# First norm of a fused mixer and expert block: its factor folded into the router's weights, its mean taken off the logits, its scale and shift applied when tokens are gathered

## The chip, the cores and the metric

The kernel runs on one core of one Trainium2 chip. The metric is the device time of one execution, in microseconds (us). Below, PE is the matrix engine, DVE the vector engine, ACT the scalar engine, POOL the general engine, and SP the engine whose queue issues most transfers. A core has 16 DMA engines.

## The reference

Two transformer blocks on 256 tokens of width 1024, all in float32. The change touches the first norm of the first block, the router that reads it and the experts that take their tokens from it:

```
h = layer_norm(ALPHA * x + mix, ln1_g, ln1_b)          # mix = concat(attn, sgu) @ w_out + b_out
logits = h @ w_router + b_router                       # 32 experts
top 4 of the logits per token; gates = softmax over the four
expert e: gt = min(h_e @ w_gate[e] + b_gate[e], 7), up = clip(h_e @ w_up[e] + b_up[e], -7, 7)
          y_e = (gt * sigmoid(1.702 gt) * (up + 1)) @ w_down[e] + b_down[e]
x2 = layer_norm(ALPHA * h + sum of gate * y_e, ln2_g, ln2_b)   # then the second block
layer_norm(r, g, b) = (r - mean) * rsqrt(var + 1e-5) * g + b
```

## The kernel before, in words

The schedule is written by hand: each engine executes its instructions in the order of the code, and waits are put in where a tile is not ready. `front` is the first mixer with the router, `moe` the experts, and a second block follows.

**Weights of the front.** `pieces` and `pump` bring weights in through a ring of raw slots. A piece is split into two float32r parts, a high part cast by ACT (L1324) and the low rest, a subtraction of two SBUF tiles on DVE or POOL (L1325). There are four half slots: when PE has used a half, `freed` gives the slot back and `pump` emits the cast and the subtraction of the next half at once, so that these stand in ACT's and DVE's order where `freed` is called. The matrix `w_out` comes as eight halves, four for output columns 0 to 511 (`wo0`) and four for 512 to 1023 (`wo1`). The `wo1` halves go into the slots that the `wo0` halves leave.

**The end of the front.** `out_half` multiplies one half for the given token tiles (t is 0 or 1, 128 tokens each): `wo0` for both tiles, `wo1` for t=0 at 512 columns, then `wo1` for t=1 twice at 256 columns (q is 0 and 256). `evict` adds the product to the residual `r` (it is `self.h`) and takes statistics. `norm` subtracts the mean and multiplies by `ln1_g` in place and computes the reciprocal root `rs` in small DVE steps. `turned` transposes a tile of `r` on PE and copies it to `hT`. `by_experts` multiplies `hT` (or one column of it) by the router's weights, `ist` sums four partial results, and `router` forms the logits, their top 8 and the normed tokens `self.x`, with `ln1_b` added by POOL (L578).

**Expert biases.** `split_biases` is a generator in three stages that turns the gate and up biases, loaded into `bf`, into three bfloat16 parts `bgu`: an ACT copy of 2048 columns and a POOL subtraction; two ACT copies that need that subtraction and a second POOL subtraction; one last ACT copy. `hT` lies in the same memory as `bf`, so the transposed rows can be written only when all three stages are over.

**Experts.** 32 experts, weights streamed through a ring of nine tiles of 2 MB that is full when `moe` begins. `gather` multiplies the tokens by one-hot columns for two experts at a time and copies the result from PSUM to `xg`, half by DVE (L756), half by ACT (L757). `start_sum`, after the third expert's gate and up, starts the accumulator with ALPHA times the tokens plus the gated `b_down`. `scatter` adds the experts' results; its first two products need the PSUM banks that the gather before it used.

The lines around the change's first loop are these:

```
        for i in range(4):
            out_half(po, range(NT), i, self.parts("wo0"))
            freed()
            if i == 0:
                next(biases, None)
        c4 = by_experts(lambda k: bqs[:, 10 + k:11 + k], 1, V.tensor_copy)
        for t in range(NT):
            evict(t, 0, po[t])
        next(biases, None)
```

Of the kernel before, what the change touches and what calls it, by code (L numbers as in the profile page):

```python
# [12 lines left out]
F32 = mybir.dt.float32  # L13
# [4 lines left out]
OP = mybir.AluOpType  # L18
# [21 lines left out]
WARM = 12, 10, 11, 20  # L40
# [31 lines left out]
class Net:  # L72
# [66 lines left out]
    def run(self):  # L139
# [30 lines left out]
        self.top = pb.tile([128, NT, 8], F32, name="top")  # L170
        with ExitStack() as fctx:
            self.front(fctx)
# [28 lines left out]
    def front(self, fctx):  # L201
# [41 lines left out]
        bst = fp.tile([18, 128], F32, name="bst")  # L243
        nc.scalar.dma_start(bst[0:10, :], b_in[0:1280].rearrange("(r c) -> r c", c=128))
        nc.scalar.dma_start(bst[10:18, :], a["ln1_b"].rearrange("o (r c) -> (o r) c", c=128))
# [69 lines left out]
        p = bank("o", [128, 18])  # L315
# [5 lines left out]
        bqs = fp.tile([128, 18], F32, name="bqs")  # L321
# [207 lines left out]
        wr, ln1g, ln1b = L["wr"], L["ln1g"], L["ln1b"]  # L529
        lst = [f2.tile([128, 4, 6], F32, tag="lst", name=self.nm("lst")) for _ in range(NT)]  # L530

        def by_experts(rhs, n, E):

            p = bank("s", [128, n])
            for k in range(KC):
                j = k % 4
                self.mm(p[32 * j:32 * j + 32, :], wr[:, k, :], rhs(k), start=k < 4, stop=k >= 4)
            o = f2.tile([128, n], F32, tag=f"le{n}", name=self.nm("le"))
            E(o, p)
            return o  # L540

        cb = fp.tile([128, NE], F32, name="cb")

        bf = L["bf"]
# [7 lines left out]

        def norm(t):

            mv = f2.tile([128, 2], F32, tag="lmv", name=self.nm("lmv"))
            V.bn_aggr(mv, lst[t])
# [6 lines left out]
        def turned(t):  # L563
            for c0 in (0, 4):
                p = bank("s", [128, 4, 128])
                for c in range(4):
                    self.tr(p[:, c, :], r[:, t, (c0 + c) * 128:(c0 + c + 1) * 128])
                S.copy(hT[:, c0:c0 + 4, t * 128:(t + 1) * 128], p)

        def router(t, rs):  # L570
            le = by_experts(lambda k: hT[:, k, t * 128:(t + 1) * 128], 128, S.copy)
            p = bank("s", [128, NE])
            self.mm(p, le, ist)
            V.scalar_tensor_tensor(self.lg[:, t, :], p, rs, cb, op0=OP.mult, op1=OP.add)
# [34 lines left out]
        for q in (0, 256):  # L609
            p = bank("mm", [128, 256])  # L610
            for i in range(4):
                out_half({1: p}, (1,), i, self.parts("wo1", 0 if q else i), slice(q, q + 256))
                if q:
                    freed()
                    if i == 1:
                        turned(0)
# [1441 lines left out]
```

## Time and profile before

| | us |
|---|---|
| median of 3 runs | 1551.1 (1549.34 to 1552.4) |
| profiled execution, its own time | 1553.83 |
| span of the profiled execution | 1552.2 |
| PE busy | 1430.2 (92% of the span) |
| DVE busy | 613.9 (40%) |
| ACT busy | 365.4 (24%) |
| POOL busy | 179.3 (12%) |

The span runs from the first to the last instruction of the one profiled execution; times in the rows below count from its start. Busy shares are means over stages that differ: the front takes about the first 124 us, the experts' weights are streamed from there to about 1035 us, and the second block fills the rest. In the rows "idle before <- X" names what ended the engine's wait. [...]

### The profile page before, as it was taken

The numbers are of one execution on the slowest core, as the hardware profiler recorded it, in microseconds if no ns is written. First come the engines' busy times: TensorE is split into PE (matmuls) and PEld (weight loads), VectorE is DVE, ScalarE is ACT, GpSimd is POOL, SyncE is SP. The second block draws the span as 40 slices with busy tenths as digits, with TensorE's granted clock in tenths as the row PEclk, the third lists the DMA queues.
The fourth block names the chain that finished last, engine by engine and source line by source line (L and its number), as shares of the span: only waits on it lengthen the run. The fifth ranks groups of instructions, "written<-read, shape, count | busy, mean of one in ns | idle before, by whom it ended". The sixth has DMA issues, their size and how long they took to land. (4 is left out here: it accounts for less than half of the span.)

```text
span 1552.2 us, 19103 instructions
## 1 busy us (share of the span) xinstructions
PE 1430.2 (92%) x7944; PEld 830.2 (53%) x7944; DVE 613.9 (40%) x1087; ACT 365.4 (24%) x607; POOL 179.3 (12%) x155
## 2 busy tenths in 40 slices
PE   8789899999999989999998989897998999999998
PEld 7674333333333333333233233237877777799998
DVE  5882131222122122122124122126597547876664
ACT  4551100010110100100100110113643323365452
POOL 4630000000000011000000000004352223200000
PEclk9999989999999999999999999998988999999999
DMA  9887999999999999999999999983423124765530
GB/s 301 286 332 293 426 409 408 428 427 427 429 427 428 428 425 421 427 429 427 429 426 428 427 427 428 428 334 116 136 89 119 32 86 169 241 220 186 195 136 28
DMA packets 94510, 491.13 MB, mean 316 GB/s; under 512 B 13639, under 2 KB 44039, under 8 KB 67284
## 3 DMA queue, kind: packets, MB, share of 16 engines
q1 hardware_dynamic: 93536, 489.01, 78.2%
q8 instruction: 64, 1.05, 0.3%
q10 hardware_dynamic: 372, 0.66, 0.1%
q0 software_dynamic: 512, 0.20, 0.1%
q14 instruction: 26, 0.21, 0.0%
HBM read 488.34 MB, written 1.51 MB: 316 GB/s over the span
## 5 line engine op out<-in xcount | busy, mean ns | idle before, releaser
L89 PE MATMUL g<-w,xg 128*64 128x512 f32 x1024 | 239.0, 620 | 6.2 <-DMA w<-in_w_gate_dram 6.2
L89 PE MATMUL u<-w,xg 128*64 128x512 f32 x1024 | 227.1, 594 | 13.6 <-DMA w<-in_w_up_dram 13.6
L89 PE MATMUL y<-w,hidT 128*64 128x512 f32 x1024 | 226.9, 595 | 2.9 <-DMA w<-in_w_down_dram 1.7
L89 PEld LDWEIGHTS u<-w,xg 128*64 128x64 f32 x1024 | 70.8, 137 | 159.4 <-issue 132.6
L89 PEld LDWEIGHTS g<-w,xg 128*64 128x64 f32 x1024 | 74.5, 143 | 150.9 <-issue 137.7
L1324 ACT CAST w<-w 128x1024 fp32r<-128x1024 f32 (+1 forms) x116 | 118.7, 1035 | 148.8 <-PE pj L89 62.0
L89 PEld LDWEIGHTS y<-w,hidT 128*64 128x64 f32 x1024 | 70.8, 137 | 152.7 <-issue 144.8
L1325 POOL TENSOR_TENSOR w<-w,w 128x1024 fp32r<-128x1024 f32 (+1 forms) x33 | 79.5, 2413 | 587.8 <-ACT w L1324 582.5
L1325 DVE TENSOR_TENSOR w<-w,w 128x1024 fp32r<-128x1024 f32 x83 | 114.0, 1390 | 83.6 <-ACT w L1324 83.6
L823 ACT COPY y<-y 64x512 f32<-64x512 f32 x64 | 37.1, 579 | 369.8 <-PE y L89 369.4
L801 DVE TENSOR_SCALAR g<-g 128x512 f32<-128x512 f32 x32 | 22.1, 691 | 220.4 <-PE g L89 220.4
L816 DVE COPY hidT<-tr 128x256 f32<-128x256 f32 x32 | 13.6, 425 | 231.7 <-ACT hidT L815 231.7
L804 DVE TENSOR_SCALAR g<-u 128x512 f32<-128x512 f32 x32 | 22.1, 692 | 172.5 <-PE u L89 172.5
L89 PE MATMUL pj<-w,h2p 128*128 128x512 f32 x336 | 84.3, 408 | 0.9 <-DVE w L1325 0.9
L802 ACT ACTIVATE sg<-g 128x512 f32<-128x512 f32 x32 | 20.2, 630 | 244.9 <-DVE g L801 244.9
L89 PEld LDWEIGHTS pj<-w,h2p 128*128 128x128 f32 x336 | 64.2, 195 | 17.3 <-DVE w L1325 1.3
L89 PE MATMUL sc<-y,ogT 128*128 128x512 f32 x124 | 62.5, 619 | 3.0 <-ACT y L823 1.4
L772 DVE TENSOR_TENSOR h<-h,sc 128x512 f32<-128x512 f32 x60 | 41.1, 687 | 28.4 <-PE sc L89 28.4
L1325 DVE TENSOR_TENSOR wp<-w,wp 128x1024 fp32r<-128x1024 f32 x32 | 38.4, 1224 | 18.6 <-ACT wp L1324 18.6
L89 PE MATMUL mm<-w,xp 128*128 128x512 f32 (+1 forms) x168 | 37.3, 383 | 6.3 <-DVE xp L329 6.3
L1065 POOL MEMSET late_scratch<- 128x128 f32 x1 | 0.2, 205 | 366.8 <-PEq L899 366.8
L89 PEld LDWEIGHTS tr<-oh,x 128*128 128x128 f32 x256 | 32.0, 203 | 17.9 <-issue 17.9
(537 smaller groups left out, 1858.9 us busy)
## 6 DMA issues: line engine op xcount, KB each, us to landing
w<-in_w_up_dram SPq DMA_DIRECT2D x58, 2048.0 KB, 32.2
w<-in_w_down_dram SPq DMA_DIRECT2D x58, 2048.0 KB, 33.8
w<-in_w_gate_dram SPq DMA_DIRECT2D x56, 2048.0 KB, 33.9
w<-in_w_in_dram SPq DMA_DIRECT2D x27, 1024.0 KB, 5.2
w<-in_w_ffn_up_dram SPq DMA_DIRECT2D x22, 1024.0 KB, 5.2
w<-in_w_gate_dram SPq DMA_DIRECT2D x16, 1024.0 KB, 11.6
w<-in_w_up_dram SPq DMA_DIRECT2D x12, 1024.0 KB, 7.3
w<-in_w_down_dram SPq DMA_DIRECT2D x12, 1024.0 KB, 13.9
```

The costliest lines, as they stand in the source:

```text
L89: return self.nc.tensor.matmul(out, lhsT, rhs, start=start, stop=stop)
L772: nc.vector.tensor_tensor(dst, dst, pp[dh], op=OP.add)
L801: nc.vector.tensor_scalar(g1, pg, 7.0, None, op0=OP.min)
L802: nc.scalar.activation(sg, g1, AF.Sigmoid, scale=1.702)
L804: nc.vector.tensor_scalar(g1, pu, -7.0, 7.0, op0=OP.max, op1=OP.min)
L816: nc.vector.tensor_copy(hidT[:, 2:4].rearrange("p j f s -> p j (f s)"), p[:, 2:4])
L823: nc.scalar.copy(yv[64 * i:64 * i + 64, hf * 512:(hf + 1) * 512], py[64 * hf:64 * hf + 64, :])
L1065: nc.gpsimd.memset(self.vstage[0], 0.0)
L1324: nc.scalar.copy(t[:, 0], src)
L1325: self.low[j % len(self.low)].tensor_tensor(t[:, 1], src, t[:, 0].bitcast(F32), op=OP.subtract)
```

## The change

The norm is no longer written out before the router. With r the residual, m its mean and rs the reciprocal root, the logits are rs * (r @ (g * w_router) - m * sum(g * w_router)) + (b @ w_router + b_router). So the tokens kept for the gather are only (r - m) * rs, made by one ACT instruction per tile with a scale and a bias (`spread`), and `ln1_g` and `ln1_b` are applied per row of the transposed tokens when the gather is evicted (`normed`), where both are columns of `norm1`. POOL's addition of `ln1_b` falls away. The rows are transposed before they are normed, in pieces between the products of `wo1`. `start_sum` takes `ln1_g` from two loads of 256 KB on POOL's queue and `ln1_b` as a 33rd row of `b_down`. The two broadcast loads of 512 KB each in the front are gone; three small loads on ACT's queue come in at the start, two of them in runs of 16 bytes. The stages of the biases are called one step earlier each, the copies of the two constant columns (`cc`) stand behind the evictions, and 12 warming products stand where 20 stood.

```diff
-WARM = 12, 10, 11, 20
+WARM = 12, 10, 11, 12
...
+        for i, nme in enumerate(("ln1_g", "ln1_b")):
+            nc.scalar.dma_start(self.norm1[:, i, :].rearrange("p (i x) -> p i x", x=4),
+                                a[nme].rearrange("o (i p x) -> p (o i) x", x=4, p=128))
...
-            L["ln1g"] = load("ln1g", [128, D], bcast_rows(a["ln1_g"], D))
-            L["ln1b"] = load("ln1b", [128, D], bcast_rows(a["ln1_b"], D))
...
+        wrg = fp.tile([128, KC, NE], F32, name="wrg")
+        V.tensor_tensor(wrg, wr, bqs[:, 18:26, None].to_broadcast([128, KC, NE]), op=OP.mult)
...
+        def turned(t, c0, n):
+
+            p = bank("s", [128, n, 128])
+            for c in range(n):
+                self.tr(p[:, c, :], r[:, t, (c0 + c) * 128:(c0 + c + 1) * 128])
+            S.copy(hT[:, c0:c0 + n, t * 128:(t + 1) * 128], p)
...
             V.bn_aggr(mv, lst[t])
-            for n in range(2):
-                rr = r[:, t, n * 512:(n + 1) * 512]
-                V.scalar_tensor_tensor(rr, rr, mv[:, 0:1], ln1g[:, n * 512:(n + 1) * 512],
-                                       op0=OP.subtract, op1=OP.mult)
-            return self.rsqrt(f2, mv[:, 1:2], 1, add=1e-5)
...
+            V.scalar_tensor_tensor(q, cb[:, 1], nm[:, 0:1], p, op0=OP.mult, op1=OP.add)
+            V.scalar_tensor_tensor(self.lg[:, t, :], q, rs, cb[:, 0], op0=OP.mult, op1=OP.add)
             V.max(self.top[:, t, :], self.lg[:, t, :])
-
-            S.activation(self.by_chunks(self.x[:, t, :]), self.by_rows(r[:, t, :]), AF.Copy, scale=rs)
-            G.tensor_tensor(self.by_chunks(self.x[:, t, :]), self.by_chunks(self.x[:, t, :]), self.by_rows(ln1b), op=OP.add)
+            V.tensor_tensor(nm[:, 1:2], nm[:, 0:1], rs, op=OP.mult)
...
         po = [bank("mm", [128, 512]) for _ in range(NT)]
+        next(biases)
         for i in range(4):
             out_half(po, range(NT), i, self.parts("wo0"))
             freed()
-            if i == 0:
-                next(biases, None)
-        c4 = by_experts(lambda k: bqs[:, 10 + k:11 + k], 1, V.tensor_copy)
+            if i == 1:
+                next(biases)
+        next(biases, None)
         for t in range(NT):
             evict(t, 0, po[t])
-        next(biases, None)
+        cc = fp.tile([128, 2], F32, name="cc")
+        V.tensor_copy(cc[:, 0:1], by_experts("b", wr, lambda k: bqs[:, 10 + k:11 + k], 1))
+        V.tensor_copy(cc[:, 1:2], by_experts("m", wrg, lambda k: self.ones[:, 0:1], 1))
...
-            if i == 1:
-                pc = bank("s", [128, NE])
-                self.mm(pc, c4.to_broadcast([128, 128]), ist)
-                V.tensor_tensor(cb, pc, L["br"], op=OP.add)
+            if i == 0:
+                pc = bank("s", [128, 2, NE])
+                for x in range(2):
+                    self.mm(pc[:, x, :], cc[:, x:x + 1].to_broadcast([128, 128]), ist)
+                V.tensor_tensor(cb[:, 0, :], pc[:, 0, :], L["br"], op=OP.add)
+                V.tensor_copy(cb[:, 1, :], pc[:, 1, :])
+            elif i > 1:
+                turned(i - 2, 0, 4)
...
+        between = {(0, 0): lambda: routed(0, 0, 4), (0, 1): lambda: turned(0, 4, 4), (0, 2): lambda: routed(1, 0, 4),
+                   (0, 3): lambda: routed(0, 4, 4), (256, 0): lambda: logits(0), (256, 1): lambda: router(0),
+                   (256, 2): lambda: turned(1, 4, 2), (256, 3): lambda: routed(1, 4, 2)}
...
+            g, b = (self.norm1[:, i, c:c + 1] for i in range(2))
+            if dve:
+                nc.vector.tensor_scalar(o, p, g, b, op0=OP.mult, op1=OP.add)
+            else:
+                nc.scalar.activation(o, p, AF.Identity, scale=g, bias=b)
...
-                nc.vector.tensor_copy(xg[b][:, c0:c0 + 2, :], p[:, 0:2])
-                nc.scalar.copy(xg[b][:, c0 + 2:c0 + 4, :], p[:, 2:4])
+                for c in range(4):
+                    normed(xg[b][:, c0 + c, :], p[:, c, :], c0 + c, c < 2)
...
+            for n in range(2):
+                nc.gpsimd.dma_start(lng[n], bcast_rows(a["ln1_g"][:, n * 512:(n + 1) * 512], 512))
...
+                    nc.vector.tensor_tensor(self.by_rows(r), self.by_chunks(self.h[:, t, cs]), self.by_rows(lng[n]),
+                                            op=OP.mult)
+                    nc.vector.scalar_tensor_tensor(r, r, ALPHA, p, op0=OP.mult, op1=OP.add)
```

ACT's order while PE multiplies `wo0`, first before the change. A cast that writes a `w` tile is the high part of one half of `wo1`, in the order 0 to 3; the casts that write `bgu` are the stages of the biases.

```order
L1324 CAST w_118<-w_117 128x1024 [waits DMAHW7_49,PE_49]
L637 CAST bgu<-bf 96x2048 [waits DMAHW3_49,DMAHW4_49,DMAHW2_49,DMAHW5_49,DMAHW1_49,DMAHW0_49]
L1324 CAST w_118<-w_117 128x1024 [waits PE_49]
L1324 CAST w_119<-w_117 128x1024 [waits DMAHW0_49,PE_49]
L1324 CAST w_119<-w_117 128x1024 [waits PE_49]
L640 CAST bgu<-bf 32x2048 [waits Pool_49]
L641 CAST bgu<-bf 32x2048
L644 CAST bgu<-bf 32x2048 [waits Pool_49]
```

The same place of ACT's order with the change:

```order
L668 CAST bgu<-bf 96x2048 [waits DMAHW4_49,DMAHW5_49,DMAHW3_49,DMAHW6_49,DMAHW2_49,DMAHW1_49]
L1372 CAST w_119<-w_118 128x1024 [waits DMAHW0_49,PE_49]
L1372 CAST w_119<-w_118 128x1024 [waits PE_49]
L671 CAST bgu<-bf 32x2048 [waits Pool_49]
L672 CAST bgu<-bf 32x2048
L1372 CAST w_120<-w_118 128x1024 [waits DMAHW1_49,PE_49]
L1372 CAST w_120<-w_118 128x1024 [waits PE_49]
L675 CAST bgu<-bf 32x2048 [waits Pool_49]
```

The two casts of the second stage, the first of which waits for POOL, moved from behind the last cast of `wo1` to ahead of its third.

DVE's order from the last part of the mixed tokens (`xp`) on, first before the change. The subtractions that write `w` tiles are the low parts of `wo1`; `h` with its statistics is `evict`; `le` is the copy of the constant column.

```order
L1325 TENSOR_TENSOR w_118<-w_117,w_118 128x1024 [waits Activation_49]
L1325 TENSOR_TENSOR w_119<-w_117,w_119 128x1024 [waits DMAHW0_49,Activation_49]
L1325 TENSOR_TENSOR w_119<-w_117,w_119 128x1024 [waits Activation_49]
L539 COPY le_903<-s_894 128x1 [waits PE_49]
L549 TENSOR_TENSOR h<-h,mm_829 128x512 [waits Pool_49]
L551 BN_STATS lst_826<-h 128x6 [waits DVE_49]
L551 BN_STATS lst_826<-h 128x6
L549 TENSOR_TENSOR h<-h,mm_830 128x512 [waits Pool_49]
L551 BN_STATS lst_827<-h 128x6 [waits DVE_49]
L551 BN_STATS lst_827<-h 128x6
```

The same place of DVE's order with the change:

```order
L1373 TENSOR_TENSOR w_119<-w_118,w_119 128x1024 [waits Activation_49]
L1373 TENSOR_TENSOR w_120<-w_118,w_120 128x1024 [waits DMAHW1_49,Activation_49]
L1373 TENSOR_TENSOR w_120<-w_118,w_120 128x1024 [waits Activation_49]
L556 TENSOR_TENSOR h<-h,mm_831 128x512 [waits Pool_49]
L558 BN_STATS lst_828<-h 128x6 [waits DVE_49]
L558 BN_STATS lst_828<-h 128x6
L556 TENSOR_TENSOR h<-h,mm_832 128x512 [waits PE_49,Pool_49]
L558 BN_STATS lst_829<-h 128x6 [waits DVE_49]
L558 BN_STATS lst_829<-h 128x6
L618 COPY cc<-s_907 128x1 [waits PE_49]
L619 COPY cc<-s_917 128x1 [waits PE_49]
```

The copy of the constants moved from ahead of the two evictions to behind them.

PE's order at the start of `wo1` for t=0, first before the change. The products that write an `mm` tile are those of `wo1`; the one that reads `ist` spreads the constants over the tokens.

```order
L89 MATMUL mm_914<-w_118,xp_760 128x512 [waits DVE_49]
L89 MATMUL mm_914<-w_118,xp_761 128x512
L89 MATMUL mm_914<-w_118,xp_760 128x512 x2
L89 MATMUL mm_914<-w_118,xp_761 128x512
L89 MATMUL mm_914<-w_118,xp_760 128x512 [waits Activation_49]
L89 MATMUL mm_914<-w_118,xp_760 128x512 [waits DVE_49]
L89 MATMUL mm_914<-w_118,xp_761 128x512
L89 MATMUL mm_914<-w_118,xp_760 128x512 x2
L89 MATMUL mm_914<-w_118,xp_761 128x512
L89 MATMUL s_927<-ist,le_903 128x32 [waits DVE_49]
L89 MATMUL mm_914<-w_119,xp_760 128x512 [waits Activation_49]
```

The same place of PE's order with the change:

```order
L89 MATMUL s_917<-ones,wrg 32x1 x7
L89 MATMUL mm_927<-w_119,xp_760 128x512 [waits Activation_49]
L89 MATMUL mm_927<-w_119,xp_760 128x512 [waits DVE_49]
L89 MATMUL mm_927<-w_119,xp_761 128x512
L89 MATMUL mm_927<-w_119,xp_760 128x512 x2
L89 MATMUL mm_927<-w_119,xp_761 128x512
L89 MATMUL s_934<-ist,cc 128x32 [waits DVE_49] x2
L89 MATMUL mm_927<-w_119,xp_760 128x512 [waits Activation_49]
```

The product with the constants moved from behind twelve products of `wo1` to behind six.

## Rows read from the trace of the kernel before

**Rows 1.** Windows: busy time per engine, granted clock, DMA share, GB/s.
```profile
115.00:120.00 5.00, 1.80 (x13) 1.54 (x13) 3.46 (x4) 1.68 (x3) 3.01 (x3) 0.85 0.05 20
...
400.00:500.00 100.00, 97.86 (x470) 36.97 (x468) 22.05 (x34) 8.97 (x18) 0.00 (x0) 0.99 1.01 427
```

**Rows 2.** Waits of PE, 124 to 1060 us: total us, times, longest.
```profile
PE u L89 <- DMA w<-in_w_up_dram: 13.6, 14, 1.3
...
PE g L89 <- DMA w<-in_w_gate_dram: 6.2, 8, 1.2
```

**Rows 3.** Timeline from the front's last product to the first expert's.
```profile
103.27 0.14 DVE L109 TENSOR_SCALAR rsw<-lmv 128x1 f32<-128x1 f32 x1
...
104.78 0.16 DVE L121 SCALAR_TENSOR_TENSOR rsi<-rst,rsi 128x1 f32<-128x1 f32 x1
...
105.80 0.42 DVE L549 TENSOR_TENSOR h<-h,mm 128x256 f32<-128x256 f32 x1
...
106.71 0.26 DVE L556 BATCH_NORM_AGGREGATE lmv<-lst 128x2 f32<-128x24 f32 x1
...
113.51 0.17 DVE L709 TENSOR_SCALAR rnmx<-top 128x2 f32<-128x2 f32 x1
...
115.07 2.78 DVE L726 TENSOR_TENSOR sel<-rgt,req 128x64 bf16<-128x64 f32 x1
...
119.08 3.39 PE L89 MATMUL tr<-oh,x 128*128 128x128 f32 x16 [0.94 <-DVE oh L744]
...
124.43 7.03 PE L89 MATMUL g<-w,xg 128*64 128x512 f32 x32
```

**Rows 4.** Timeline, ACT and POOL during wo0: start, us, what.
```profile
83.86 0.62 ACT L328 CAST xp<-w 128x512 fp32r<-128x512 f32 x1 [2.14 <-DVE w L524]
...
85.54 1.90 ACT L637 CAST bgu<-bf 96x2048 bf16<-96x2048 f32 x1
...
87.57 4.11 POOL L638 TENSOR_TENSOR bf<-bf,bgu 96x2048 f32<-96x2048 f32 x1 [8.84 <-issue]
...
92.99 1.05 ACT L1324 CAST w<-w 128x1024 fp32r<-128x1024 f32 x1 [1.75 <-PE mm L89]
```

**Rows 5.** Timeline, DVE from 88 to 98 us.
```profile
88.47 4.30 DVE L1325 TENSOR_TENSOR w<-w,w 128x1024 fp32r<-128x1024 f32 x1 [1.57 <-ACT w L1324]
...
94.07 1.23 DVE L1325 TENSOR_TENSOR w<-w,w 128x1024 fp32r<-128x1024 f32 x1 [0.17 <-ACT w L1324]
95.21 0.15 DVE L539 COPY le<-s 128x1 f32<-128x1 f32 x1
95.28 0.68 DVE L549 TENSOR_TENSOR h<-h,mm 128x512 f32<-128x512 f32 x1
...
97.37 0.75 DVE L551 BATCH_NORM_STATS2 lst<-h 128x6 f32<-128x256 f32 x2
```

**Rows 6.** Windows while wo0 and the first gather run: granted clock third from last.
```profile
82.00:84.00 2.00, 2.00 (x7) 1.52 (x6) 1.73 (x3) 0.14 (x1) 0.00 (x0) 0.50 1.00 414
120.00:122.00 2.00, 2.00 (x12) 2.00 (x11) 0.00 (x0) 0.00 (x0) 0.00 (x0) 0.51 0.03 8
```

**Rows 7.** Timeline, PE from 96 to 106 us.
```profile
96.15 7.32 PE L89 MATMUL mm<-w,xp 128*128 128x512 f32 x48
...
103.30 1.03 PE L93 MATMUL s<-ident,h 128*128 128x128 f32 x8
...
105.69 0.64 PE L89 MATMUL s<-bf,wr 128*32 128x128 f32 x16
```

**Rows 8.** DMA issues: queue, count, KB each, us from issue to landing.
```profile
wr<-in_w_router_dram SPq DMA_DIRECT2D x1, 128.0 KB, 10.5
...
qkg<-in_k_norm_g_dram POOLq DMA_DIRECT2D x1, 32.0 KB, 9.5
```

**Rows 9.** Groups by line: the gather's copy on ACT, 130 to 1030 us, and a biased ACT copy.
```profile
L757 ACT COPY xg<-sc 128x256 f32<-128x256 f32 x15 | 5.6, 372 | 22.5 <-DVE xg L756 22.5
...
L382 ACT ACTIVATE w<-mm,bqs x4: 465/468/471, 23.0 to 32.2; 128x256 f32<-128x256 f32 x4
```

More of the change, by code (lines that the diff above doesn't have):

```diff
@@ L170, in run @@
         self.top = pb.tile([128, NT, 8], F32, name="top")
+        self.norm1 = pb.tile([128, 2, KC], F32, name="norm1")
         with ExitStack() as fctx:
@@ L242, in front @@
         b_in = a["b_in"][0]
-        bst = fp.tile([18, 128], F32, name="bst")
+        bst = fp.tile([26, 128], F32, name="bst")
         nc.scalar.dma_start(bst[0:10, :], b_in[0:1280].rearrange("(r c) -> r c", c=128))
-        nc.scalar.dma_start(bst[10:18, :], a["ln1_b"].rearrange("o (r c) -> (o r) c", c=128))
+        for i, nme in enumerate(("ln1_b", "ln1_g")):
+            nc.scalar.dma_start(bst[10 + 8 * i:18 + 8 * i, :], a[nme].rearrange("o (r c) -> (o r) c", c=128))
+        for i, nme in enumerate(("ln1_g", "ln1_b")):
+            nc.scalar.dma_start(self.norm1[:, i, :].rearrange("p (i x) -> p i x", x=4),
+                                a[nme].rearrange("o (i p x) -> p (o i) x", x=4, p=128))
         spec, halves = [], []
@@ L313, in front @@
                         pattern=[[-1, 128]], channel_multiplier=1)
-        p = bank("o", [128, 18])
+        p = bank("o", [128, 26])
         self.tr(p, bst)
@@ L526, in front, with by_experts @@
         through("c0", "c2", "c3", "c4")
-        wr, ln1g, ln1b = L["wr"], L["ln1g"], L["ln1b"]
+        wr = L["wr"]
+        wrg = fp.tile([128, KC, NE], F32, name="wrg")
+        V.tensor_tensor(wrg, wr, bqs[:, 18:26, None].to_broadcast([128, KC, NE]), op=OP.mult)
         lst = [f2.tile([128, 4, 6], F32, tag="lst", name=self.nm("lst")) for _ in range(NT)]
-        def by_experts(rhs, n, E):
-            p = bank("s", [128, n])
-            for k in range(KC):
-                j = k % 4
[L537 to L542, printed above, removed]
+        pe, le, pl = {}, {}, {}
+        def by_experts(key, w, rhs, n, ks=range(KC)):
+            if key not in pe:
+                pe[key] = bank("s", [128, n])
+            for k in ks:
+                j = k % 4
+                self.mm(pe[key][32 * j:32 * j + 32, :], w[:, k, :], rhs(k), start=k < 4, stop=k >= 4)
+            return pe[key]
+        cb = fp.tile([128, 2, NE], F32, name="cb")
         bf = L["bf"]
@@ L551, in evict, with routed @@
                 V.bn_stats(lst[t][:, 2 * n + (q + x) // 256, :], rr[:, x:x + 256])
+        def turned(t, c0, n):
[3 more added lines that the diff above has]
+            S.copy(hT[:, c0:c0 + n, t * 128:(t + 1) * 128], p)
+        def routed(t, c0, n):
+            by_experts(t, wrg, lambda k: hT[:, k, t * 128:(t + 1) * 128], 128, range(c0, c0 + n))
+            if c0 + n == KC:
+                le[t] = f2.tile([128, 128], F32, tag="le", name=self.nm("le"))
+                S.copy(le[t], pe[t])
@@ L553, in norm, with logits @@
+        def logits(t):
+            pl[t] = bank("s", [128, NE])
+            self.mm(pl[t], le[t], ist)
         def norm(t):
             mv = f2.tile([128, 2], F32, tag="lmv", name=self.nm("lmv"))
+            nm = f2.tile([128, 2], F32, tag="lnm", name=self.nm("lnm"))
             V.bn_aggr(mv, lst[t])
-            for n in range(2):
-                rr = r[:, t, n * 512:(n + 1) * 512]
-                V.scalar_tensor_tensor(rr, rr, mv[:, 0:1], ln1g[:, n * 512:(n + 1) * 512],
-                                       op0=OP.subtract, op1=OP.mult)
@@ L561, in norm @@
-            return self.rsqrt(f2, mv[:, 1:2], 1, add=1e-5)
[L563 to L574, printed above, removed]
+            V.tensor_scalar(nm[:, 0:1], mv[:, 0:1], -1.0, None, op0=OP.mult)
@@ L578, in router, with spread @@
-            G.tensor_tensor(self.by_chunks(self.x[:, t, :]), self.by_chunks(self.x[:, t, :]), self.by_rows(ln1b), op=OP.add)
+            V.tensor_tensor(nm[:, 1:2], nm[:, 0:1], rs, op=OP.mult)
+        def spread(t):
+            rs, nm = fac[t]
+            S.activation(self.by_chunks(self.x[:, t, :]), self.by_rows(r[:, t, :]), AF.Identity, scale=rs, bias=nm[:, 1:2])
         biases = self.split_biases(bf[0:96].rearrange("p (q c) -> p q c", q=2))
@@ L614, in front @@
                     freed()
-                    if i == 1:
-                        turned(0)
+                between.get((q, i), lambda: None)()
             evict(1, 1, p, q, 256)
-        fac[1] = norm(1)
-        router(0, fac[0])
-        turned(1)
-        router(1, fac[1])
+            if q:
+                turned(1, 6, 2)
+                routed(1, 6, 2)
+                logits(1)
+                spread(0)
+                fac[1] = norm(1)
+                router(1)
+                spread(1)
         self.warm(bank("o", [128, 128]), self.ident, WARM[3])
@@ L918, in overflow @@
                             self.mm(p[:, k, :], self.h[:, t, k * 128:(k + 1) * 128], oh[:, t], start=t == 0, stop=t == NT - 1)
-                    nc.vector.tensor_copy(xo, p)
+                    for k in range(KC):
+                        normed(xo[:, k, :], p[:, k, :], k, True)
                     def weights(nme):
```

31 lines of the change are left out of this document (19 added, 12 removed).

## The prediction

> **What bounds the kernel now.** I read the busy shares of the page, then windows by stage, then PE's waits, then the timeline of the stage that the change rewrites. The experts are paced by the weight stream. From 400 to 500 us the DMA engines are full at 427 GB/s [rows 1], and PE waits for weights 19.8 us over the stage in these two groups alone [rows 2]. But between 115 and 120 us the stream stands still, with a DMA share of 0.05 [rows 1]: the ring is full and no slot comes free before the first expert's first product at 124.43 us [rows 3]. So the start of that product (call it G) starts the stream again, everything behind it is moved by as much as G is, and what PE loses later, inside the stream, is paid from its 19.8 us of waits. The question is what the change does to G.
>
> **The chain to G, before.** PE ends `wo1` and DVE evicts its last piece at 105.80. From there to the gather at 119.08 is a DVE chain of 13.3 us, and the gather takes 5.35 more [rows 3]. In the chain `sel` takes 2.78 us for 64 columns, where steps of its kind take some 0.2: POOL is adding `ln1_b` then. That hold is the same that a low part of `wo1` shows at 88.47, 4.30 us instead of 1.23, while POOL's subtraction runs from 87.57 to 91.68 [rows 4, 5]. It ended 1.1 us after POOL did, so a DVE instruction with two SBUF inputs stands until POOL is done. Evictions read PSUM, and at 95.28 one takes 0.68.
>
> **What the change saves behind the last product.** The chain becomes: eviction, statistics and their joining 105.80 to 106.97, 1.2; the negated mean 0.2; the eight steps of the root 103.27 to 104.94, 1.7; two logit steps, the top 8 and the product of mean and root, four at about 0.2 with their gaps, 0.9; the choice, 113.51 to 115.07, 1.55; `sel` 0.2 now that POOL is silent; `sel`'s end (117.85) to the gather (119.08), 1.25 [rows 3]. The sum is 7.0 instead of 13.3, so 6.3 saved. The other branches fit in: the last transposes, copies and products of t=1 take some 2.4 and end before the root does, and ACT's two `spread` instructions end near 6.3. The first gather ran at 0.51 of the clock [rows 6] after PE had waited for `sel`. With the shorter wait I take the full clock, 4.15 instead of 5.35 (bounds 3.8 and 5.35), 1.2 saved. 12 warming products suit that gap, so their cut costs nothing; if the clock falls all the same, the 1.2 is gone.
>
> **What it costs ahead of it: a wait of PE for the constants.** The order says this, and durations come from the rows.
> ACT: the last part of `xp` ends at 84.48 [rows 4]. The biases' first cast is now next, to 86.4; the casts of `wo1` halves 0 and 1 follow, to 88.5. Then stands a cast that waits for POOL's subtraction, 86.4 plus 4.1, so 90.5. Two bias casts of 1.90 end at 94.3, and halves 2 and 3 of `wo1` are cast by 95.4 and 96.4. Before, the last of these casts began at 92.99, when PE freed the slot.
> POOL: its second subtraction starts behind those bias casts, 94.3, and ends at 98.4.
> DVE: the low part of half 2 is due at 95.4, inside that subtraction, and is held as at 88.47: done at 98.4 plus 1.1, 99.5. Half 3, 1.23, 100.7. Only now the two evictions of `wo0`, 95.28 to 98.12 before, 2.84 [rows 5]: 103.6. Behind them the two copies of 0.15 into `cc`: 103.9. Before, the one copy came at 95.21, ahead of the evictions.
> PE: `wo0` ends at 92.95 [rows 4], two small products 0.6, six products of `wo1`. The 48 at 96.15 are 12 wide and 36 half as wide, 7.32 us for 30 wide ones, 0.244 each [rows 7]: 95.1. Then comes the product with `cc`, ready at 103.9. **PE stands for 8.8 us**, and everything on PE is queued behind it. No cover: nothing else is ahead of it in PE's order.
>
> **From there to the last product.** Before, 96.15 to 105.80 was 9.65 us: 12 wide and 48 half-wide products and 8 transposes. Now six wide products more, 1.5; six transposes more at 1.03 for 8, 0.8; three half-sets of router products, 24 at 0.64 for 16, 1.0; logits and constants about 0.6 [rows 3, 7]. That is 13.5. After an idle stretch PE begins at half clock: 0.50 at 82 to 84 us, after it had waited for the tokens, and 0.51 at 120 [rows 6]. At half clock an interval of work takes twice its time, so 2 us of such running, as one of these rows has, costs 1.0, the bounds are 1.0 and 2.6, half of the gather's 5.35, and I take 2.0. The last product is evicted at 103.9 + 13.5 + 2.0 = 119.4 instead of 105.8. G = 119.4 + 7.0 + 4.15 = 130.6 against 124.4: **+6.1**.
>
> **Inside the experts.** The two loads of `ln1_g` bring 512 KB into a full stream: at 427 GB/s +1.2 [rows 1]. The 1 MB that leaves the front leaves a stretch in which the ring fills anyway: 0. `start_sum` needs the first of these loads: issued when the third expert's swiglu ends, landing perhaps as late as 9.5 us, the slowest of the small loads by POOL's queue [rows 8]; that is about 1.3 us behind the moment when its first eviction could go, and half of it falls in PE's own pace there: +0.5 (bounds 0 and 3).
> [...]
> The gather's evictions double in number. An ACT copy of 256 columns takes 0.372, one with a bias 0.468 [rows 9], so two of 128 columns lie between 0.372 and 0.94; DVE's likewise between its 0.425 and twice that. Upper bound 1.0 us a gather, in front of the scatter that needs the bank, 15 in all. PE's waits for weights, 19.8, cover it; without that cover it is up to 15. Only the first gather with a scatter comes before the stream is behind PE: +0.5.
> At the start, 512 runs of 16 bytes go in beside the first weights. No row shows such runs; the router's load, 1,024 runs of 128 bytes, landed in 10.5 us, one of 32 KB by POOL's queue in 9.5 [rows 8]. Bounds 0 and 1; I take 0, since ACT is busy with casts of `x` when the first weights land.
>
> **Sum.** +6.1 +1.2 +0.5 +0.5 = +8.3 on the profiled 1553.83, 1562.1. That execution lies 2.7 above the median of the runs, so on the median 1551.1 + 8.3 = 1559.4; I say 1559. With the bounds of clock, gather and loads its own range is 1556.5 to 1563.
>
> **Rivals.** *PE does not stand for the constants* (ends on the other side: faster). If the casts of `wo1` came no later than before, the 8.8 and the 2.0 fall away: 8.3 - 10.8 = -2.5, 1548.5. Speaks for it: all savings behind the last product stay, and POOL's additions are really gone. Against it: in DVE's order the copies stand behind the evictions, and the cast that waits for POOL stands ahead of half 2. The case turns where wait and slow clock together are under 2.5 us. Chance 0.13.
> *DVE is not held by the second subtraction*: half 2 is done at 96.6, half 3 at 97.9, `cc` at 101.0, 2.9 less, 1556.3. For it: the hold needs POOL to be first, by 1.1 us here. Against it: 4.30 at 88.47. Chance 0.17. [...]
> *`start_sum` waits in full* for the loads, or the evictions are not covered: +3 more, 1562.5. Chance 0.1.
> *It moves nothing*: the stream's restart is not tied to G, or savings and wait cancel, 1551 to 1553. Against it stands the idle stream at 115 to 120. Chance 0.1.
>
> **How the numbers follow.** The forecast has 0.5, the rivals 0.13, 0.17, 0.1 and 0.1. A measurement of this kernel tells about 0.2%, 3.1 us, from no change. Faster takes the first rival, 0.13; same takes the last and a little of the second, 0.13; slower the rest, 0.74. The range 1551 to 1564 leaves out the first rival and the tail above the third, together less than 0.2.
>
> **What would show it.** In the trace after: ACT's cast of `wo1` half 2 near 94 instead of 90; DVE's subtraction of it stretched to some 4 us under POOL's second subtraction; PE idle 8 to 9 us before the product with `cc`, released by DVE, and half a clock behind it; no 2.78 us `sel`; gather 7 us behind the last eviction; G near 130.6. Wrong would be: no wait of PE there, or a G that moves while the end doesn't.

## The result, and the profile after

| | before | changed |
|---|---|---|
| median of 6 runs each, us | 1550.22 (1544.77 to 1552.4) | 1560.53 (1556.26 to 1564.18) |
| ratio to before, 95% interval | | 1.0071 (1.0047 to 1.0096) |
| span of the profiled execution, us | 1552.2 | 1562.6 |

The changed kernel is slower by 0.71%, which is 11.0 us (the ratio is that of the means; the medians differ by 10.3). Of the 10.4 us between the two spans, 9.6 stand before the weight stream starts again. SP's queue shows it: the first row is the transfer into the slot that PE frees last in `wo0`, the last row the first refill of the ring in the experts. Of the kernel before:

```profile
92.79 11.51 SPq L1312 DMA_DIRECT2D w<-in_w_up_dram  x4
...
126.36 0.33 SPq L690 DMA_DIRECT2D w<-in_w_down_dram  x1
```

Of the changed kernel, the same queue:

```profile
92.62 26.36 SPq L1360 DMA_DIRECT2D w<-in_w_up_dram  x4
...
136.00 0.33 SPq L721 DMA_DIRECT2D w<-in_w_down_dram  x1
```

From the first row to the last it is 33.57 us before and 43.38 after. That stretch is the measure of every experiment below, since the end of `wo0` itself lies between 91.16 and 94.59 us in the twelve profiled executions. Where the time went is seen on the engines of that stretch, here ACT, POOL and DVE in the timeline after (start, duration, engine, line, operation, count; in brackets the idle time before and its releaser):

```profile
90.40 1.90 ACT L671 CAST bgu<-bf 32x2048 bf16<-32x2048 f32 x1 [1.98 <-POOL bf L669]
...
94.24 1.99 ACT L1372 CAST w<-w 128x1024 fp32r<-128x1024 f32 x2
94.35 4.06 POOL L673 TENSOR_TENSOR bf<-bf,bgu 32x2048 f32<-32x2048 f32 x1 [3.98 <-ACT bgu L672]
95.32 5.31 DVE L1373 TENSOR_TENSOR w<-w,w 128x1024 fp32r<-128x1024 f32 x2 [2.73 <-ACT w L1372]
100.55 0.67 DVE L556 TENSOR_TENSOR h<-h,mm 128x512 f32<-128x512 f32 x1
...
103.30 0.14 DVE L618 COPY cc<-s 128x1 f32<-128x1 f32 x1
```

The chain reads downward. ACT waits for POOL (90.40), its casts of `wo1` halves 2 and 3 come only at 94.24 (before, the last began at 92.99 [rows 4]), DVE's two low parts take 5.31 us for a work of 2 times 1.23 [rows 5] while POOL subtracts, the evictions come at 100.55 instead of 95.28, and the constants behind them at 103.30. PE's rows at the same place, first of the kernel before:

```profile
93.12 3.05 PE L89 MATMUL mm<-w,xp 128*128 128x512 f32 x12
96.01 0.30 PE L89 MATMUL s<-ist,le 128*128 128x32 f32 x2
```

The same place in the changed kernel:

```profile
93.22 1.67 PE L89 MATMUL mm<-w,xp 128*128 128x512 f32 x6
103.50 1.06 PE L89 MATMUL s<-ist,cc 128*128 128x32 f32 x4 [8.61 <-DVE cc L618]
```

PE stands for 8.61 us in front of the product with the constants, where before it came to that product without a wait. Then the clock is at its lower level for some 4.9 us of work, as the windows show (the granted clock is the third number from the end, 1.00 at full speed; in the first gather of the kernel before PE ran 12 products in the 2 us from 120 at 0.51 and 12 in the 1 us from 123 at 1.00); the windows behind the dots are the first gather:

```profile
104.00:106.00 2.00, 2.00 (x7) 1.71 (x7) 0.29 (x2) 0.00 (x0) 0.00 (x0) 0.50 0.41 172
106.00:108.00 2.00, 2.00 (x6) 1.52 (x6) 0.00 (x0) 0.00 (x0) 0.00 (x0) 0.50 0.00 0
108.00:110.00 2.00, 2.00 (x12) 1.63 (x11) 0.00 (x0) 0.22 (x1) 0.00 (x0) 0.90 0.00 0
...
128.00:130.00 2.00, 1.57 (x9) 1.57 (x10) 0.38 (x1) 0.00 (x0) 0.00 (x0) 0.72 0.86 365
130.00:132.00 2.00, 2.00 (x11) 2.00 (x11) 0.08 (x1) 0.00 (x0) 0.00 (x0) 0.50 0.05 16
132.00:134.00 2.00, 2.00 (x18) 1.87 (x18) 0.71 (x3) 0.80 (x2) 0.00 (x0) 0.92 0.00 0
```

The end of the stretch, from the last eviction to the first product of the first expert:

```profile
119.83 0.42 DVE L556 TENSOR_TENSOR h<-h,mm 128x256 f32<-128x256 f32 x1 [1.63 <-PE mm L89]
...
121.95 4.12 ACT L597 ACTIVATE x<-h,lnm,rsi 128x1024 f32<-128x1024 f32 x2
...
125.05 0.23 DVE L757 TENSOR_TENSOR sel<-rgt,req 128x64 bf16<-128x64 f32 x1
...
126.09 1.28 ACT L742 ACT_TABLE_LOAD   x1
127.39 0.53 ACT L742 ACTIVATE rex<-lg,rnmx 128x32 f32<-128x32 f32 x2
127.95 0.43 DVE L775 TENSOR_TENSOR oh<-rk,slot 128x256 f32<-128x256 f32 x1 [2.11 <-ACT rex L742]
128.43 3.39 PE L89 MATMUL tr<-oh,x 128*128 128x128 f32 x16 [2.85 <-DVE oh L775]
...
134.07 6.17 PE L89 MATMUL g<-w,xg 128*64 128x512 f32 x28
```

`sel` takes 0.23 us instead of 2.78 [rows 3], as POOL is silent. But the one-hot columns `oh` now wait 2.11 us for ACT's exponentials, which stand behind the two spreads (4.12 us) and a table load (1.28). And the first gather, from 128.43 to 134.07, takes 5.64 us, some 3.4 of it at the low clock. The prediction's sum had neither; the second it named as a condition. The first expert's product comes 9.64 us later than before (134.07 against 124.43 [rows 3]), just as the refill does. Inside the experts, PE's waits from 124 to 1060 us (total us, times, longest), as in [rows 2]:

```profile
PE u L89 <- DMA w<-in_w_up_dram: 14.3, 13, 1.2
PE sc L89 <- DVE h L811: 10.3, 14, 0.8
PE g L89 <- DMA w<-in_w_gate_dram: 5.0, 5, 1.2
```

At the scatter PE now waits 10.3 us (1.0 in the kernel before). The scatter needs the bank that the slower eviction of the gather frees late (ACT's part of the first such bank takes 0.80 us at 132.76, 0.37 at 122.97 in the kernel before); the profile names DVE's addition, which ends at nearly the same moment (in one scatter at 287.65, ACT's eviction at 287.73). The waits for weights are 19.3 us against 19.8 for the same two groups.

### The profile page after: what moved, and what is told of

It reads as the page before. It is cut to its first block, busy times and chain, and to the rows that moved or that the text cites. A ratio compares the mean times of both kernels' runs of the same rounds, so it can differ in the third digit from the quotient of the medians.

```text
span 1562.6 us, 19213 instructions
## 1 busy us (share of the span) xinstructions
PE 1421.7 (91%) x7946; PEld 825.2 (53%) x7946; DVE 620.9 (40%) x1129; ACT 379.3 (24%) x640; POOL 174.3 (11%) x155
## 5 line engine op out<-in xcount | busy, mean ns | idle before, releaser
L89 PE MATMUL g<-w,xg 128*64 128x512 f32 x1024 | 235.1, 612 | 5.0 <-DMA w<-in_w_gate_dram 5.0
L89 PE MATMUL sc<-y,ogT 128*128 128x512 f32 x124 | 62.5, 619 | 11.7 <-DVE h L811 10.3
L785 ACT ACTIVATE xg<-tr,norm 128x128 f32<-128x128 f32 x32 | 12.9, 453 | 145.3 <-DVE xg L783 145.3
L89 PE MATMUL mm<-w,xp 128*128 128x512 f32 (+1 forms) x168 | 41.1, 400 | 6.3 <-DVE xp L333 6.3
L89 PEld LDWEIGHTS sc<-y,ogT 128*128 128x128 f32 x124 | 20.0, 189 | 45.6 <-DVE h L811 32.8
```

The costliest lines, as they stand in the source:

```text
L89: return self.nc.tensor.matmul(out, lhsT, rhs, start=start, stop=stop)
L785: nc.scalar.activation(o, p, AF.Identity, scale=g, bias=b)
```

## Experiments

Each is compared with the kernel before on the same chip. The column "to refill" is the stretch from the end of `wo0` to the first refill in each profiled execution, as read above. The last column is the ratio's excess over 1, times 1551 us.

| kernel | ratio (95% interval) | PE's wait at the constants, us | to refill, us | against 33.57 | by the ratio, us |
|---|---|---|---|---|---|
| changed kernel | 1.0071 (1.0047 to 1.0096) | 8.61 | 43.38 | +9.8 | +11.0 |
| 1 constants late | 1.0040 (1.0027 to 1.0054) | none | 38.60 | +5.0 | +6.2 |
| 2 second stage late | 1.0044 (1.0029 to 1.0058) | 3.26 | 37.50 | +3.9 | +6.8 |
| 3 no second subtraction | 1.0064 (1.0050 to 1.0078) | 6.15 | 41.30 | +7.7 | +9.9 |
| 4 both late | 1.0029 (1.0019 to 1.0039) | none | 37.00 | +3.4 | +4.5 |
| 5 maxima in their own place | 1.0059 (1.0040 to 1.0077) | 8.75 | 39.57 | +6.0 | +9.2 |
| 6 plain gather | 1.0082 (1.0067 to 1.0098) | 8.78 | 43.22 | +9.7 | +12.7 |
| 7 both late, rows apart | 1.0006 (0.9996 to 1.0016) | none | 32.22 | -1.4 | +0.9 |
| 8 as 7, maxima in their own place | 0.9977 (0.9965 to 0.9990) | none | 28.30 | -5.3 | -3.6 |
| 9 as 8, no loads of `ln1_g` | 0.9978 (0.9964 to 0.9991) | none | 28.61 | -5.0 | -3.4 |
| 10 before, early stages | 1.0053 (1.0035 to 1.0072) | 4.72 | 40.53 | +7.0 | +8.2 |

The last two columns move together over 15 us, with the second 1 to 3 us above the first in every line. Why it lies above isn't shown; the first column rests on one execution of each kernel, and run 10, which has none of the new work in the experts, shows 1.2 of it. In the twelve profiled executions the first refill comes between 119.46 and 136.00 us, and the time from it to the end of the span is 1421.5 to 1428.1 us, in no order with it. So the end follows the first refill about one to one, which the prediction took from the idle stream, and the rival in which it doesn't falls.

**1. The product with the constants three quarters of `wo1` later.**

```diff
-            if i == 0:
+            if i > 1:
+                turned(i - 2, 0, 4)
+            if i == 3:
                 pc = bank("s", [128, 2, NE])
...
-            elif i > 1:
-                turned(i - 2, 0, 4)
```

> The product with the two constant columns moves from behind the first quarter of wo1 (t=0) to behind the fourth. My theory: PE stood 8.6 us there because DVE was late, and nothing else on PE needed DVE's evictions yet. Now PE waits only for the low part of half 2, which DVE finishes near 99.4 us, so about 2.7 us from 96.7 us on; the wait shrinks by 5.6 to 6, and the half clock behind it (2.5 us lost) may go too. First product of the first expert at 126 to 128.3 us instead of 133.9, median 1552.4 to 1555. Rival, the stream's restart does not set the end: first product earlier by as much, median still 1560.

PE's wait is now for the low part of half 2, and a small one for the eviction that the transposes need:

```profile
100.10 1.44 PE L89 MATMUL mm<-w,xp 128*128 128x512 f32 x5 [3.35 <-DVE w L1373]
101.92 1.08 PE L93 MATMUL s<-ident,h 128*128 128x128 f32 x4 [0.39 <-DVE h L556]
```

The two waits sum to 3.74 instead of 8.61, and the last eviction came 21.3 us behind the end of `wo0` instead of 27.2. The first product came at 129.81, later than expected: the half clock stayed behind the shorter wait too (0.50 from 102 to 104 us), and this execution's first gather took 6.7 us. The ratio, 1.0040, is above the 1.0014 to 1.0031 that the expected medians make. The constants were a cause, not the only one.

**2. The biases' second stage behind all casts of `wo1`.**

```diff
-            if i == 1:
+            if i == 3:
                 next(biases)
-        next(biases, None)
         for t in range(NT):
             evict(t, 0, po[t])
+        next(biases, None)
```

> The second stage of the biases is called behind all casts of wo1 (after the fourth quarter of wo0), the third behind the evictions. My theory: the casts of halves 2 and 3 no longer stand behind the cast that waits for POOL, their low parts end near 95.2 us, the evictions near 98.1 and the copies of the constants near 98.4, so PE waits 3.3 to 3.6 us for the constants instead of 8.6, and the median falls by 5 to 7.6 to 1553 to 1555.5. Rival, the evictions and DVE's own load make the wait and not ACT's order: wait stays above 7 us, median 1559 to 1561.

The wait was 3.26 us and the refill 5.9 us sooner in the stretch, as the theory of ACT's order has it. POOL's second subtraction starts at 99.40 us here, behind all low parts, so this run takes the hold of DVE out together with ACT's order. The rival, DVE's own load, is out. The median fell less than expected, by 4.2 us of the 5 to 7.6 (1.0071 to 1.0044), within what the two intervals allow.

**3. Without POOL's second subtraction.**

```diff
-        nc.gpsimd.tensor_tensor(bf[64:96], bf[64:96], bgu[64:96], op=OP.subtract)
```

> POOL's second subtraction of the biases is left out, so the third part of the biases is wrong; all else stands where it stood. Theory of the hold (a DVE instruction with two SBUF inputs stands while POOL works on SBUF): the low part of half 2 takes 1.2 us instead of 4.1, everything behind it comes 2.9 us sooner, PE waits 5.7 us, median 1557.6 or less. Rival, the 4 us of that low part have another cause (ACT's writes, the stream): wait stays 8.6, median 1560.5.

The third part of the biases is then no longer what it should be; all else stands in its place. DVE's low parts in its timeline, the first two under POOL's first subtraction, the others now with POOL silent:

```profile
87.75 5.49 DVE L1372 TENSOR_TENSOR w<-w,w 128x1024 fp32r<-128x1024 f32 x2 [1.73 <-ACT w L1371]
95.96 2.36 DVE L1372 TENSOR_TENSOR w<-w,w 128x1024 fp32r<-128x1024 f32 x2 [2.72 <-ACT w L1371]
```

2.36 us for two instead of 5.31, and the wait of PE fell from 8.61 to 6.15. The hold by POOL is shown, with 2.5 us (PE's wait) to 3.0 (DVE's two low parts) as its price here, and with it the rival that DVE isn't held falls. In the stretch to the refill 2.1 us of it are left, since the clock behind the wait was at 0.50 for some 6.8 us in this execution instead of 4.9. The ratio fell by 1.1 us, less than the expected 2.9; the two intervals leave room for either.

**4. Both moves.**

> Both moves together. My theory: PE finds every half of wo1 and the constants ready, no wait over 1 us from the end of wo0 to the last product and full clock there, so the last eviction comes near 109 us instead of 119.8, the first expert's product near 122.8 instead of 133.9, median 1549.4, at or just below the kernel before. Rivals: the late third stage of the biases keeps the memory of the transposed rows and PE waits 3 us or more for them, median 1553 or more; or the end is not tied to the first product, median 1560.

The wait for the constants is gone, and the first rival took its place, on the very memory that it named. PE and ACT in that kernel:

```profile
101.62 0.53 PE L89 MATMUL s<-ist,cc 128*128 128x32 f32 x4
...
106.54 0.57 PE L89 MATMUL s<-bf,wrg 128*32 128x128 f32 x8 [3.60 <-issue]
```

```profile
103.93 1.89 ACT L675 CAST bgu<-bf 32x2048 bf16<-32x2048 f32 x1 [4.26 <-POOL bf L673]
105.86 1.07 ACT L565 COPY bf<-s 128x512 f32<-128x512 f32 x2
```

The copy of the transposed rows (105.86) writes the memory of the biases, so it stands behind their third stage, which waits 4.26 us for POOL; the router's product waits 3.60 us for it. So the early stages of the change have a use: either the casts of `wo1` or the rows stand behind POOL, as long as both share these tiles and queues.

**5. The maxima in a place of their own.**

```diff
-        nmx = rp.tile([128, NT], F32, name="rnmx")
+        nmx = mp.tile([128, NT], F32, name="rnmx")
```

> The changed kernel with one tile moved: the negated maxima of the router (rnmx) get a place of their own, so that the first one-hot columns (oh), which lay over them, no longer wait for ACT's exponentials. My theory of the 1.6 us that the tail took beyond my sum: ACT's two spreads (4.12 us), the table load (1.28) and the exponentials (0.53) end at 127.95, and oh waited for them 2.1 us. Then oh follows the ranks at 125.85 us, the gather starts 8.0 us - 2.1 = 6.4 us behind the last eviction instead of 8.6, the gap of PE in front of it shrinks from 2.9 to 0.8 us and its half clock may go (1.2 us). First product of the first expert 2.1 to 3.4 us sooner, ratio to the kernel before 1.005 to 1.006 instead of 1.007. Rival, the gather needs the spread rows as late: nothing moves, ratio 1.007.

DVE, ACT and PE in the timeline of that kernel:

```profile
126.03 0.43 DVE L775 TENSOR_TENSOR oh<-rk,slot 128x256 f32<-128x256 f32 x1
...
126.61 2.02 PE L89 MATMUL tr<-oh,x 128*128 128x128 f32 x16 [0.87 <-DVE oh L775]
...
130.59 0.59 PE L89 MATMUL g<-w,xg 128*64 128x512 f32 x2
```

`oh` no longer waits, the gather starts 6.6 us behind the last eviction (119.99), and it takes 3.98 us at full clock (1.00 from 126 to 130 us). The stretch to the refill fell by 3.8 us, more than the 2.1 to 3.4 of the theory, and the ratio to 1.0059, whose interval doesn't tell it from 1.0071 by itself; runs 7 and 8 differ by the same edit and their intervals lie apart.

**6. The gather evicted as before.**

```diff
-                for c in range(4):
-                    normed(xg[b][:, c0 + c, :], p[:, c, :], c0 + c, c < 2)
+                nc.vector.tensor_copy(xg[b][:, c0:c0 + 2, :], p[:, 0:2])
+                nc.scalar.copy(xg[b][:, c0 + 2:c0 + 4, :], p[:, 2:4])
```

> The changed kernel with the gather's evictions as before (two copies of 256 columns a bank, without the norm's factor and shift, which are thereby left out). My theory: the 0.7 us that each of the 15 later gathers takes longer is paid from PE's waits for weights, only the first gather and the first scatter show it: 0.5 to 1 us less, ratio 1.0065. Rival, they are on the path: 0.7 times 15 = 10 us less, ratio 1.000.

This leaves the norm's scale and shift out of the experts' tokens. Nothing was gained, ratio 1.0082, where 0.5 to 1 us less was expected; the intervals of the two ratios overlap. The scatter's wait falls from 10.3 us to 1.0, and the waits for weights are 18.8 us instead of 19.3:

```profile
PE u L89 <- DMA w<-in_w_up_dram: 12.7, 11, 1.4
PE g L89 <- DMA w<-in_w_gate_dram: 6.1, 8, 1.3
```

No part of the slower eviction shows in the time. But it is not PE's waits for weights that pay for it, since these hardly change. It is PE's other work that takes less time: from the first refill to the second block's load of `norm_g` (the first window below is the changed kernel's, the second this run's) PE is busy 823.89 us with the slower eviction and 832.20 without, for the same number of products (3893):

```profile
136.00:1032.86 896.86, 823.89 (x3893) 307.94 (x3890) 201.75 (x384) 98.58 (x204) 14.63 (x48) 0.98 1.00 424
136.00:1032.18 896.18, 832.20 (x3893) 309.64 (x3890) 192.63 (x354) 85.11 (x174) 14.62 (x48) 0.98 1.00 425
```

Summed over windows of 2 us, the clock was at its lower level for about 31 us of that stretch in the changed kernel, 44 in this run and 41 in the kernel before; why it differs isn't shown. The DMA engines are full in both (share 1.00), and the two stretches are nearly as long (896.86 and 896.18 us).

**7. Both late, and the rows apart.** To the edits of runs 1 and 2 (the third stage now behind `wo1` of t=0) comes a tile for the first half of the transposed rows; there is room for half of them only.

```diff
-        hT = bf.rearrange("p (k t) -> p k t", k=KC)
+        hA = fp.tile([128, 4, T], F32, name="hA")
+        hB = bf[:, 0:4 * T].rearrange("p (k t) -> p k t", k=4)
...
+        next(biases, None)
         evict(0, 1, p)
```

> Constants late and the second stage of the biases late, as in the run of both together, and the first half of the transposed rows in memory of its own, with the third stage behind wo1 of t=0. My theory: PE now waits neither for constants nor for rows; the last eviction comes 15.8 us behind the end of wo0 (before 13.0, changed kernel 27.2, both late 21.1), the first expert's product 14 us later, 29.8 us behind the end of wo0 against 31.6 before: 1.8 us sooner, which the loads inside the experts take back by half. Ratio 0.9995 (0.998 to 1.0005). Rival, that the reordered front costs more than its waits show: ratio stays at 1.003.

The stretch is 32.22 us and the ratio 1.0006, the time of the kernel before within its interval. The front lost its waits for the constants and the rows, and with them some 10 of the 11 us; the wait of `oh` is still there (2.85 us in front of the gather).

**8. The same, with the maxima in a place of their own.**

> The same with the maxima in a place of their own: 2.1 us sooner yet, and 1.2 more if the first gather runs at full clock. First expert's product 26.5 to 27.7 us behind the end of wo0, ratio 0.998 (0.997 to 0.9993), faster than both kernels. Rival: the experts give back what the front saves, ratio 1.000 or above.

The stretch is 28.30 us (5.3 less than before), the ratio 0.9977 (0.9965 to 0.9990). This version is faster than both kernels. The places that cost, in its timeline:

```profile
98.03 0.53 PE L89 MATMUL s<-ist,cc 128*128 128x32 f32 x4
...
99.28 0.43 PE L89 MATMUL s<-hA,wrg 128*32 128x128 f32 x8
...
106.94 0.42 DVE L557 TENSOR_TENSOR h<-h,mm 128x256 f32<-128x256 f32 x1 [1.63 <-PE mm L89]
...
113.56 2.02 PE L89 MATMUL tr<-oh,x 128*128 128x128 f32 x16 [0.87 <-DVE oh L777]
```

The constants and the rows have no wait in front of them, the clock stays full (1.00 from 96 to 100 us and from 114 to 116), and the last eviction comes 15.8 us behind the end of `wo0`. From the last eviction to the gather it is 6.6 us.

**9. Without the loads of `ln1_g` inside the experts.** The edit is in `start_sum`, on the kernel of run 8; DVE fills the tiles with ones, so the scale is left out of the residual sum.

```diff
-                nc.gpsimd.dma_start(lng[n], bcast_rows(a["ln1_g"][:, n * 512:(n + 1) * 512], 512))
+                nc.vector.memset(lng[n], 1.0)
```

> The version with the rows apart and the maxima in their own place, without the two loads of ln1_g inside the experts: the tiles are filled with ones by DVE, so the scale is left out of the residual sum. My sum had 1.2 us for their 512 KB in the full stream and 0.5 for the wait of start_sum. If so, the stretch from the first refill of the ring to the loads of the second block, 895.8 us in the version with the loads, gets 1.2 to 1.7 us shorter, ratio 0.9967 instead of 0.9977. Rival, the bytes are paid from time in which no transfer was due anyway: the stretch stays within 0.5 us of 895.8, ratio 0.9977.

The ratio is that of run 8, and the stretch from the first refill to the second block's load of `norm_g` was not shorter. SP's queue of run 8, then of this one:

```profile
119.46 0.33 SPq L723 DMA_DIRECT2D w<-in_w_down_dram  x1
...
1015.26 0.33 SPq L1085 DMA_DIRECT2D w<-in_norm_g_dram  x1
```

```profile
121.61 0.33 SPq L723 DMA_DIRECT2D w<-in_w_down_dram  x1
...
1019.88 0.33 SPq L1085 DMA_DIRECT2D w<-in_norm_g_dram  x1
```

895.80 us with the loads and 898.27 without. In the profiled executions of all twelve kernels it lies between 895.7 and 898.4 (895.92 before, 896.86 in the changed kernel), so single executions scatter by more than the 1.2 us in question. There is no sign of that cost; by this scatter and the two intervals an amount under about 3 us stays open.

**10. The kernel before with the early stages alone.**

```diff
+        next(biases)
         for i in range(4):
             out_half(po, range(NT), i, self.parts("wo0"))
             freed()
-            if i == 0:
-                next(biases, None)
+            if i == 1:
+                next(biases)
+        next(biases, None)
...
-        next(biases, None)
         fac = {}
...
-        next(biases, None)
         fac[0] = norm(0)
```

> The kernel before with one thing of the change: the stages of the biases are called at the changed kernel's places. My theory: ACT's casts of wo1 halves 2 and 3 now stand behind the bias cast that waits for POOL, DVE's low parts of them end near 99.5 and 100.7 us, the copy of the constants right behind them at 100.9, and PE waits 4 to 4.5 us in front of the product with the constants, which stands there behind the second quarter of wo1; with 0 to 2 us of half clock the first expert's product comes at 128.5 to 131 us instead of 124.4, ratio 1.003 to 1.004. Rival, the order of the biases costs nothing without the moved rows: ratio 1.000.

ACT, POOL, DVE and PE in its timeline:

```profile
92.58 1.90 ACT L641 CAST bgu<-bf 32x2048 bf16<-32x2048 f32 x1
...
94.50 2.00 ACT L1324 CAST w<-w 128x1024 fp32r<-128x1024 f32 x2
94.62 4.08 POOL L642 TENSOR_TENSOR bf<-bf,bgu 32x2048 f32<-32x2048 f32 x1 [3.99 <-ACT bgu L641]
95.58 5.33 DVE L1325 TENSOR_TENSOR w<-w,w 128x1024 fp32r<-128x1024 f32 x2 [2.73 <-ACT w L1324]
...
100.84 0.14 DVE L539 COPY le<-s 128x1 f32<-128x1 f32 x1
...
101.04 0.64 PE L89 MATMUL s<-ist,le 128*128 128x32 f32 x2 [4.72 <-DVE le L539]
```

Row for row what the changed kernel showed, without any of its new arithmetic. The order of the biases alone costs the kernel before 8.2 us by the ratio and 7.0 us up to the refill: 4.7 of wait, and the clock at 0.50 from 101 to 105 us behind it, 2.0 lost. That is more than the expected ratio of 1.003 to 1.004, which had 0 to 2 us of half clock.

## Why the prediction came out

The forecast was 1559 and the range 1551 to 1564; the median was 1560.53. Its steps:

- **What bounds it.** Right. The end follows the first refill about one to one over the whole table, and the fourth rival falls.
- **PE stands for the constants.** Predicted 8.8 us from 95.1 to 103.9, measured 8.61 from 94.9 to 103.50. The members of the chain were taken out in turn: the wait is 8.61 us with all of them, 6.15 without POOL's hold of DVE (run 3), 3.26 with neither the hold nor ACT's order (run 2), and none with the product later as well (run 4). The first rival (no wait) and the second (no hold) fall. What spoke for the second, that the hold needs POOL to be first, does show in the kernel before: DVE's subtraction at 60.70 us began 0.24 us ahead of POOL's L499 (60.94, 1.87 us) and took 1.20 us. Runs 7 and 10 are the same cause taken out of the one kernel and put into the other.
- **From the constants to the last eviction.** Predicted 13.5 of work and 2.0 of half clock, 15.5; measured 16.3 (103.50 to 119.83). By the windows about 4.9 us ran at the low level, which is 2.4 us lost of the 16.3. The last eviction was predicted for 119.4 and came at 119.83.
- **What the change saves behind the last product.** This term was mis-sized. Predicted 7.0 us from the last eviction to the gather and 4.15 for the gather, a saving of 7.5 together; measured 8.60 and 5.64, a saving of 4.4. The DVE chain itself was right: `sel` came 5.2 us behind the last eviction, and when `oh` waits for nothing the 7.0 is 6.6 (runs 5 and 8). The sentence that failed is "The other branches fit in": I followed ACT as far as its spreads, to 6.3 us behind the last eviction (they ended at 6.2), and not to the table load and the exponentials behind them, on which `oh` waits for the memory of `rnmx`. That is 2.1 us. The clock then fell all the same, by the condition that the sum had named, and the 1.2 was gone: gathers behind a gap of about 2.85 us took 5.4 to 6.7 us, those behind 0.87 us 3.97 to 3.98 (runs 5, 8 and 9).
- **Inside the experts.** Predicted +2.2; in the one profiled pair +0.9 (refill +9.64, loads of the second block +10.58). The gather's eviction costs no time, as the sum had it, but not for the reason that the sum gave: PE's waits for weights, which were to cover it, are 19.3 us with it and 18.8 without, and what shrank is PE's busy time, by 8.3 us (run 6). `start_sum`'s first load landed 8.1 us after its issue and the second 10.5, around the 9.5 that was taken from a row, and DVE waited 1.3 us for the first; from the copy of `gT` to the next gate product it took 7.90 us against 7.62 before, so 0.3 of the 0.5. The third rival, with 3 us more, falls as far as this pair shows. The 1.2 for the bytes isn't seen (run 9).
- **The start.** The runs of 16 bytes show no cost: the end of `wo0` came at 92.62 against 92.79. As this moment moves by up to 3.4 us between executions, a cost of the bound of 1 us would not be seen.

So the sum of 8.3 was close to the 10.4 of the profiled executions partly by luck, because two errors had opposite signs: the front was 3.5 us worse than forecast (0.4 up to the last eviction, 1.6 from there to the gather, 1.5 in the gather) and the experts some 1.3 better. The bounds that the sum names for clock, gather and loads add up to about 1557.5 to 1563.7 and not to 1556.5 to 1563; the median lies in both. The interval of the ratio (7.3 to 14.9 us) holds both numbers.

## What to carry to other kernels

When a step is called earlier on a queue, read what stands behind it there, and whether its own releaser is an engine that also holds others up: here a cast that waits for POOL was put ahead of casts that PE needs, and three engines passed the delay on. Follow every engine of a shortened chain to its end, including waits for the memory of short-lived tiles; a shorter chain uncovers them one after another. When a sum stands on an idle transfer stream, measure each variant from one fixed event to the moment when the stream starts again: the rows of single profiles show which wait has taken another's place, where the intervals of the ratios overlap (runs 1, 2 and 4). A single stretch scatters too, here by the clock of the first gather, so one execution doesn't settle one microsecond. And where work is said to be covered, look for what pays: here it was not the wait that had been named.

## What was not expected of the hardware

A plain subtraction of two SBUF tiles on DVE (1.23 us) under a POOL subtraction of 4.06 to 4.11 us ended 1.0 to 1.1 us after POOL had ended, in the kernel before, the changed one and run 10 alike: nearly all of its own 1.23 us came behind POOL's end, so it stood rather than shared. The prediction's sentence that such an instruction stands until POOL is done is wider than these rows, in which POOL's work has two inputs too: beside POOL's scaling of `x`, with one input (L339, 9.83 to 12.62 us in the kernel before), two such subtractions on DVE took 1.83 us (from 10.12) and 1.21 (from 11.88), the first slower than 1.23 but not held to POOL's end. Evictions from PSUM beside POOL's subtraction took 0.68 to 0.69 us (the kernel before at 99.22, run 8 at 98.80), as they did without it (0.68 at 95.28 [rows 5]); the prediction's row at 95.28 had no POOL work beside it.

Behind idle stretches of PE of 3.3 to 8.6 us the granted clock was 0.50 for 3 to 7 us (runs 1 to 3, 10 and the changed kernel); in run 4, behind 3.60 us, six half-wide products took 1.65 us instead of 0.95. Behind the gap of 0.87 us in run 5 it stayed at 1.00, where the first gather of the kernel before ran at 0.51 behind a gap of 0.94 that followed one of 2.26. Which of the two gaps set it there was not separated.
